# SBUF pools laid out anew: TensorE's operands at multiples of 1024 bytes, the small tables in a pool of their own

## The chip, the core and the metric

The kernel runs on one core of a Trainium2 chip. The metric is device time in microseconds (us), the median over several runs. One further run was taken with the hardware profiler on; its trace is what is read below. In that trace PE is TensorE (PEld its weight loads), DVE is VectorE, ACT is ScalarE, POOL is GpSimd, SP is SyncE. `L185` is line 185 of the kernel. A matmul's *stationary* operand is the one that is loaded as weights, its *moving* operand the one that is streamed through.

## What is computed

One decoder layer, batch 1, 512 tokens, width 1024, float32. Two token mixers work side by side, dilated attention and a state-space model (SSM); their outputs are gated and projected, and a SwiGLU feed-forward network with 2816 hidden channels follows.

```
p = x @ w_in                    # q, k, v (3 groups x 8 heads x 64) | ssm input | gate logits
attn = merge of 3 dilated sliding-window attentions
y_s  = glu(gelu(s5_ssm(u)));    y_attn = attn @ w_attn_br;   y_ssm = y_s @ w_ssm_br
mixed = sigmoid(g0) * y_attn + sigmoid(g1) * y_ssm
h = layer_norm(alpha * x + mixed @ w_out)
x = layer_norm(alpha * h + (silu(h @ w_ff_gate) * (h @ w_ff_up)) @ w_ff_down)
```

## The kernel before

Every large product is made of three float32r matmuls (`mm3`, L184 to L187): each float32 operand is split into a high and a low part (ACT rounds the high part, L178, DVE takes the rest, L179), and hi x hi, hi x lo, lo x hi are accumulated in one PSUM bank. Nearly all of these matmuls have 128 stationary columns and 512 moving columns ("full width"); those of the v projection of two attention groups, of the first two feed-forward tiles and of the last down product have 256 ("half width"). By the program, 3,104 matmuls are full width. The order on every engine is written out by hand.

Weights stream from HBM in units of 128 x 2048 floats, each split into two pieces of 1024 columns. A piece sits in a slot, a pair of tiles `whi{n}`, `wlo{n}`. Slots 0, 1 and 2 belong to the pool `wp`. When the pool `pa` with the tiles of the mixers is closed (L1017), the pools `pb` and `bt` are opened in its place, and slots 3 and 4 are added from `pb` (L1022). From then on the slots are used in turn, 0, 1, 2, 3, 4. The stages that the prediction speaks of, in their order in time:

- **Branch products** (L990 to L1004): eight pieces of 24 matmuls; the first four have `gh`, `gl` as moving operand, the last four `ath` (twice in every three) and `atl`.
- **Output projection** (L1065 to L1117): `mix_hi`, `mix_lo` are stationary, the weights move; one of its eight pieces lies in slot 3.
- **Feed-forward, gate and up** (`fg`, L1125 to L1160): the weight pieces are stationary, the tokens `hh`, `hl` move. A piece makes one bank: 8 k-slices x 3 = 24 matmuls. The first four pieces are done in token halves (half width), the other 40 at full width: 960 matmuls.
- **Down product** (`dn`, L1172 to L1206): the hidden channels `ff` are stationary and the weight pieces move; 18 pieces of 4 token tiles x 2 column halves x 3 = 24 matmuls, then 72 more by token tile, 504 in all at full width; the last token tile is done at half width (`dq`).

A tile pool hands out addresses in the order in which its tiles are first asked for, and each pool begins where the one before it ends. Before, the pool `cp` holds only the identity matrix (512 bytes in a partition) behind a few constants, and `pa` mixes small tables (192, 64, 512, 640, ... bytes) with large tiles.

Of the kernel before, what the change touches and what calls it, by code (L numbers as in the profile page):

```python
# [10 lines left out]
F32 = mybir.dt.float32  # L11
# [5 lines left out]
P = 128  # L17
# [6 lines left out]
NH = 8  # L24
NPAIR = 4
NG = 32
NGP = 16
# [124 lines left out]
def emit(ctx, tc, i, out):  # L152
# [3 lines left out]
    cp = ctx.enter_context(tc.tile_pool(name="cp", bufs=1))  # L156
# [40 lines left out]
    pa_ctx = ExitStack()  # L197
    pa = pa_ctx.enter_context(tc.tile_pool(name="pa", bufs=1))
    at = pa_ctx.enter_context(tc.tile_pool(name="at", bufs=2))

    def big(n, name, dt=F32):
        return pa.tile([P, 2048], dt, tag=f"big{n}", name=name)

    def gat(n, name, dt=F32):
        return pa.tile([P, 2048], dt, tag=f"gat{n}", name=name)

    def home(n, name, dt=F32):
        return gat(n[1:], name, dt) if isinstance(n, str) else big(n, name, dt)
# [22 lines left out]
        w.add(i["w_dn"][f], 1)  # L231

    warm = at.tile([P, 512], F32, tag="tv", name="warm")
    wact = at.tile([P, 1], F32, tag="wact", name="wact", bufs=1)
    xr = [big(4 + j, f"x_raw{j}") for j in range(2)]
    xp = act_pair("x")
    wu = [big(j, f"wu_raw{j}").rearrange("p (k c) -> p k c", k=4) for j in range(2)]
    wup = [[home(j, f"wu{n}{j}", F32R).rearrange("p (k c) -> p k c", k=4) for j in js] for n, js in (("h", (3, 6)), ("l", (7, "g3")))]
    small = pa.tile([P, 3, NGP], F32, name="small")
    ident = cp.tile([P, P], F32, name="ident")  # L240

    act.dma_start(small, i["ssm_small"])
    dve.memset(warm, 0.0)
# [18 lines left out]

    rope = pa.tile([P, 2, 512], F32, name="rope")
    masks = pa.tile([P, 2, 256], F32, name="masks")
    bgate = pa.tile([P, 16], F32, name="bgate")
    prep = gat(0, "prep")
    sm = prep[:, 0:1024].rearrange("p (a r e) -> p a r e", a=2, r=2)
    zt = prep[:, 1024:2048]
    dmat = pa.tile([P, 8, 16], F32, name="dmat")
    sp.dma_start(sm, i["ssm_bc"])  # L270
    w.load()
    sp.dma_start(dmat, i["dmat"])
# [11 lines left out]
    def t16():  # L284
        return t16s[:, next(n16), :]
# [94 lines left out]
    def bc(a, n):  # L380
        return a.unsqueeze(2).broadcast_to([P, NGP, n])

    ptmp = pa.tile([P, 2, NGP, 4], F32, name="ptmp")

    def powers(t, eng):
        for n0 in (1, 2, 4):
# [6 lines left out]

    are, aim, ldt = (small[:, j, :] for j in range(3))
    dtt, er, cr, ci, den, w0, w1, w2, w3, w4 = (t16() for _ in range(10))
    pw = pa.tile([P, 2, NGP, 5], F32, name="pw")
    a4 = pa.tile([P, 2, NGP, 9], F32, name="a4")
    a32 = pa.tile([P, 2, NGP, 5], F32, name="a32")
    neg = pa.tile([P, 3, NGP], F32, name="neg")
    pwn = pa.tile([P, NGP, 4], F32, name="pwn")  # L400
    ar1, ai1 = pw[:, 0, :, 1], pw[:, 1, :, 1]
    la, lb = Later(dve), Later(dve)
    exp16(dtt, ldt, la)
# [90 lines left out]
            act.copy(pf[:, 512 * q : 512 * (q + 1)], b)  # L494

    kdr = dr.tile([NG, 16, 112], F32, name="kdr")
    zer = pa.tile([16, 1, 48], F32, name="zer")
    pool.memset(zer, 0.0)
    act.dma_start(kdr.rearrange("g h e -> h g e")[:, :, 0:48], zer.broadcast_to([16, NG, 48]))

# [73 lines left out]
            act.copy(ssm["s", r][:, :, 8 * m + half : 8 * m + 8 : 2].rearrange("p s g b -> p g b s"),  # L574
                     b.rearrange("p (g b s) -> p g b s", g=4, b=16))

    f1 = pa.tile([P, 2, 4, NGP], F32, name="f1")
    e1 = pa.tile([P, 2, NGP], F32, name="e1")
    e2 = pa.tile([P, 2, NGP], F32, name="e2")

    def scan():

# [104 lines left out]
        sp.dma_start(ssm["ych"].rearrange("p (q t) -> p q t", q=4), ydr.rearrange("(q p) t -> p q t", p=P))  # L687


    st = [pa.tile([P, 2, 4, NH], F32, name=f"st{j}") for j in range(2)]  # L690
    oa = [None, None]

    def qk_tile(dv, ws, g, hp, name, mid):
# [326 lines left out]
    pb = ctx.enter_context(tc.tile_pool(name="pb", bufs=1))  # L1020
    bt = ctx.enter_context(tc.tile_pool(name="bt", bufs=2))
# [5 lines left out]
    xn = [ffslot(f"xn{j}").rearrange("p (t d) -> p t d", t=2) for j in range(2)]  # L1027
    lnb = ffslot("lnb").rearrange("p (e d) -> p e d", e=2)
    hn = pb.tile([P, NTT, D], F32, name="hn")
    epsb = pb.tile([P, 1], F32, name="epsb")  # L1030
    pool.memset(epsb, -0.5)

    def rstd(mv):
# [261 lines left out]
def build(inputs):  # L1295
    import concourse.bacc as bacc

    a = {k: np.asarray(v) for k, v in inputs.items()}
    arrays = {f"in_{k}": np.ascontiguousarray(v) for k, v in {**layout(a), **constants()}.items()}
    nc = bacc.Bacc("TRN2", target_bir_lowering=False, num_devices=1)  # L1300
    aps = {k[3:]: nc.dram_tensor(k, v.shape, mybir.dt.from_np(v.dtype), kind="ExternalInput").ap()
           for k, v in arrays.items()}
    out = nc.dram_tensor("out_dram", (S, D), F32, kind="ExternalOutput").ap()
    with tile.TileContext(nc) as tc:
        with ExitStack() as ctx:
            with tc.manual_schedule():
                emit(ctx, tc, aps, out)
    return nc, arrays
# [8 lines left out]
```

## Time and profile before

| | |
|---|---|
| median of 3 runs | 880.92 us (880.84 to 882.03) |
| profiled execution, its own time | 883.05 us |
| its span, first to last instruction | 881.3 us |
| PE busy | 865.2 us, 98% of the span, 4814 matmuls |
| DVE, ACT, POOL busy | 496.4, 294.3, 26.0 us |
| mean granted TensorE clock | 0.994 |

Matmuls overlap: a row's duration is longer than the distance to the next one's start. What a matmul costs in a row of many is the distance from start to start, here called its pitch.

### The profile page before, as it was taken

What the parts mean: (1) busy time and instruction counts of PE and PEld (TensorE: products, weight loads), DVE (VectorE), ACT (ScalarE), POOL (GpSimd) and SP (SyncE); (2) the same over time, 40 slices, a digit from 0 to 9 for tenths busy, and PEclk for the clock granted to TensorE, in tenths of its full rate; (3) what the DMA queues carried; (4) which work ended last, traced back from release to release, by engine and by line L of the source; (5) the groups of instructions that cost most, each with busy time, mean ns of one, the idle gap of its engine ahead of it and who ended that gap; (6) DMA issues with size and microseconds to landing.
All of it is one profiled execution on the core that took longest, in us unless ns stands there. A gap on an engine that the chain in (4) does not pass through costs nothing.

```text
span 881.3 us, 11787 instructions
## 1 busy us (share of the span) xinstructions
PE 865.2 (98%) x4814; PEld 715.7 (81%) x4814; DVE 496.4 (56%) x950; ACT 294.3 (33%) x479; POOL 26.0 (3%) x27
## 2 busy tenths in 40 slices
PE   9999999999999999998999999999999999999995
PEld 6878888888778897876788898888888888888885
DVE  7966899874664635366766864444444444222236
ACT  5363222254443343553233232222222222211110
POOL 0000000000000000000000410000000000000004
PEclk9999999999999999998999999999999999999999
DMA  9823421324221212112216222222222222322204
GB/s 330 188 80 103 119 96 63 129 64 134 93 96 49 96 48 100 55 43 95 96 49 267 115 95 102 95 97 97 96 94 96 98 96 95 142 95 97 92 1 96
DMA packets 23864, 90.11 MB, mean 102 GB/s; under 512 B 5722, under 2 KB 10330, under 8 KB 14722
## 3 DMA queue, kind: packets, MB, share of 16 engines
q1 hardware_dynamic: 22226, 86.87, 29.1%
q10 hardware_dynamic: 1584, 2.48, 0.8%
q8 instruction: 38, 0.62, 0.3%
q14 instruction: 16, 0.13, 0.0%
HBM read 84.92 MB, written 4.42 MB: 101 GB/s over the span
## 4 chain that ended last, share of the span: by engine, by line
PE 45%; issue 41%; DVE 8%; ACT 3%; POOL 2%; DMA 1%; SPq 0%; DVEq 0%; POOLq 0%; ACTq 0%
PE pg L185 3%; PE pg L186 3%; PE pg L187 3%; PE pv L185 3%; PE pu L548 3%; PE pv L187 3%; PE pv L186 3%; PE pk L185 3%; PE pq L185 3%; PE pq L187 2%; PE pk L187 2%; PE pq L186 2%; PE pk L186 2%; PE s L747 2%; DVE wlo L179 2%
## 5 line engine op out<-in xcount | busy, mean ns | idle before, releaser
L179 DVE TENSOR_TENSOR wlo<-raw,whi 128x1024 fp32r<-128x1024 f32 x134 | 164.1, 1228 | 203.4 <-ACT whi L178 203.2
L178 ACT CAST whi<-raw 128x1024 fp32r<-128x1024 f32 x134 | 139.6, 1046 | 217.5 <-PE dn L187 74.8
L185 PE MATMUL fg<-hh,whi 128*128 128x512 f32 (+1 forms) x384 | 143.5, 374 | 0.0
L187 PE MATMUL fg<-hh,wlo 128*128 128x512 f32 (+1 forms) x384 | 143.4, 373 | 0.0
L186 PE MATMUL fg<-hl,whi 128*128 128x512 f32 (+1 forms) x384 | 143.4, 373 | 0.0
L186 PEld LDWEIGHTS fg<-hl,whi 128*128 128x128 f32 x384 | 72.3, 188 | 13.3
L187 PEld LDWEIGHTS fg<-hh,wlo 128*128 128x128 f32 x384 | 72.3, 188 | 13.3
L185 PEld LDWEIGHTS fg<-hh,whi 128*128 128x128 f32 x384 | 72.3, 188 | 13.3
L185 PE MATMUL dn<-whi,ff 128*128 128x512 f32 x168 | 66.0, 393 | 0.0
L187 PE MATMUL dn<-whi,ff 128*128 128x512 f32 x168 | 65.9, 392 | 0.0
L186 PE MATMUL dn<-wlo,ff 128*128 128x512 f32 x168 | 65.8, 392 | 0.0
L185 PE MATMUL pg<-x_hi,whi 128*128 128x512 f32 x128 | 50.8, 397 | 0.0
L187 PE MATMUL pg<-x_hi,wlo 128*128 128x512 f32 x128 | 49.9, 390 | 0.0
L186 PE MATMUL pg<-x_lo,whi 128*128 128x512 f32 x128 | 49.9, 389 | 0.0
L181 ACT ACTIVATE ff<-fth 128x512 fp32r<-128x512 f32 x22 | 14.0, 635 | 101.6 <-DVE fth L297 101.6
L759 ACT ACTIVATE pt<-pt,st 128x256 f32<-128x256 f32 (+1 forms) x64 | 31.0, 485 | 47.1 <-DVE st L757 47.1
L297 DVE TENSOR_TENSOR fth<-fth,fg 128x512 f32<-128x512 f32 x22 | 15.1, 688 | 55.8 <-PE fg L187 55.6
L185 PE MATMUL pq<-x_hi,whi 128*128 128x512 f32 x96 | 37.9, 395 | 0.0
L185 PE MATMUL pk<-x_hi,whi 128*128 128x512 f32 x96 | 37.8, 394 | 0.0
L187 PEld LDWEIGHTS dn<-whi,ff 128*128 128x128 f32 x168 | 31.5, 188 | 7.3
L187 PE MATMUL pk<-x_hi,wlo 128*128 128x512 f32 x96 | 37.4, 390 | 0.0
L186 PE MATMUL pk<-x_lo,whi 128*128 128x512 f32 x96 | 37.4, 390 | 0.0
(254 smaller groups left out, 1564.7 us busy)
## 6 DMA issues: line engine op xcount, KB each, us to landing
raw<-in_w_in SPq DMA_DIRECT2D x26, 1024.0 KB, 4.8
raw<-in_w_gu SPq DMA_DIRECT2D x22, 1024.0 KB, 4.7
raw<-in_w_dn SPq DMA_DIRECT2D x11, 1024.0 KB, 4.8
raw<-in_w_br SPq DMA_DIRECT2D x4, 1024.0 KB, 4.7
raw<-in_w_out SPq DMA_DIRECT2D x4, 1024.0 KB, 4.7
raw<-in_w_glu SPq DMA_DIRECT2D x2, 1024.0 KB, 4.8
xn<-in_x SPq DMA_DIRECT2D x2, 1024.0 KB, 8.3
out_dram<-hn SPq DMA_DIRECT2D x13, 128.0 KB, 2.4
```

Of the source, the lines that this page charges most:

```text
L178: act.copy(hi, src)
L179: dve.tensor_tensor(lo, src, hi.bitcast(F32), op=ALU.subtract)
L181: act.mul(hi, src, scale)
L185: pe.matmul(dst, a[0], b[0], start=first, stop=False)
L186: pe.matmul(dst, a[0], b[1], start=False, stop=False)
L187: pe.matmul(dst, a[1], b[0], start=False, stop=last)
L297: eng.tensor_tensor(o, a, b, op=op)
L548: pe.matmul(bs[e], wk[a], xk[b], start=(k + a + b == 0), stop=(k == KT - 1 and a == 1))
L747: pe.matmul(banks[hh][:, 256 * j + 128 * c : 256 * j + 128 * (c + nk)], z[0][rows, hp, qs], z[1][rows, hp, 128 * k0 : 128 * (k0 + nk)], st ...
L759: act.activation(pt[:, :n], pt[:, :n], AF.Exp, bias=mneg, scale=-1.0, accum_out=zsum)
```

## The change

The instructions of PE, DVE, ACT and SP stay the same, in the same order and with the same waits; where tiles lie in SBUF changes. Three small tables (`pw`, `a32`, `e1`) move into `cp` ahead of the identity, so that `cp` ends at a round address and all pools after it begin there. All other small tables move from `pa` into a new pool `sa` behind `pa` and `at`. The one-column tile `epsb` moves from `pb` to `bt`, so that `pb`'s slots 3 and 4 follow at round addresses.

```diff
     at = pa_ctx.enter_context(tc.tile_pool(name="at", bufs=2))
+    sa = pa_ctx.enter_context(tc.tile_pool(name="sa", bufs=1))
+    pw = cp.tile([P, 2, NGP, 5], F32, name="pw")
+    a32 = cp.tile([P, 2, NGP, 5], F32, name="a32")
+    e1 = cp.tile([P, 2, NGP], F32, name="e1")
+    ident = cp.tile([P, P], F32, name="ident")
...
-    wact = at.tile([P, 1], F32, tag="wact", name="wact", bufs=1)
+    wact = sa.tile([P, 1], F32, name="wact")
...
-    small = pa.tile([P, 3, NGP], F32, name="small")
-    ident = cp.tile([P, P], F32, name="ident")
+    small = sa.tile([P, 3, NGP], F32, name="small")
...
-    bgate = pa.tile([P, 16], F32, name="bgate")
+    bgate = sa.tile([P, 16], F32, name="bgate")
...
-    dmat = pa.tile([P, 8, 16], F32, name="dmat")
+    dmat = sa.tile([P, 8, 16], F32, name="dmat")
...
-    epsb = pb.tile([P, 1], F32, name="epsb")
+    epsb = bt.tile([P, 1], F32, name="epsb", bufs=1)
```

`ptmp`, `a4`, `neg`, `pwn`, `zer`, `f1`, `e2` and `st` go from `pa` to `sa` in the same way.

Where the built programs place the tiles that TensorE reads (byte within a partition, and what is left over 128 and over 1024):

```
tile                            before   mod 128  mod 1024     after   mod 1024
ident                            16512         0       128     17920        512
whi0, wlo0 ... wlo2 (wp)         33408 ...     0       640     34816 ...      0
x, mix, ff7 to ff10 (ap_)        57984 ...     0       640     59392 ...      0
hh, hl, ff0 to ff6               90752 ...     0       640     92160 ...      0
gh                              162688         0       896    163840          0
ath (also zs, hst1, v1)         185024        64       704    182272          0
gl (also ut, q1)                194688         0       128    190464          0
whi3, wlo3, whi4, wlo4 (pb)     197280 ...    32       672    198656 ...      0
vt (at)                         215200        32       160    210944          0
pt (at)                         223392 ...    32       160    219136 ...      0
```

Slices of these tiles that a full-width matmul reads begin at multiples of 512 bytes from the tile's start (stationary) or 2048 (moving). Of the 3,104 full-width matmuls before, 700 have one operand that begins off a multiple of 128 bytes. Of the tiles before, none begins at a multiple of 256 bytes.

On POOL the waits stand elsewhere, since `epsb` now lies over other tiles than before. Its instructions from the last one of the mixers to the first layer normalization, before (`whl` is a table of the attention merge, `mva` the statistics of a token tile, `hn` its rows, `lnb` the scale and shift):

```order
L838 MEMSET whl 40x1024 [waits DMAHW2_49,DMAHW3_49,DMAHW1_49,DMAHW4_49,DMAHW0_49,DMAHW5_49,DVE_49,DMAHW6_49,PE_49,Activation_49]
L1031 MEMSET epsb 128x1 [waits DMAHW3_49,DMAHW2_49,DMAHW4_49,DMAHW1_49,DMAHW5_49,DMAHW0_49,DMAHW6_49,DVE_49,DMAHW7_49,PE_49,Pool_49]
L1035 ISA
L1035 TENSOR_TENSOR mva_4299<-mva_4299,epsb 128x1 [waits DVE_49,Pool_49]
L1059 TENSOR_TENSOR hn<-hn,lnb 128x512 [waits DMAHW2_49,Activation_49]
L1060 TENSOR_TENSOR hn<-hn,lnb 128x512 [waits Pool_49]
```

The same six on POOL in the changed program:

```order
L842 MEMSET whl 40x1024 [waits DMAHW2_49,DMAHW3_49,DMAHW1_49,DMAHW4_49,DMAHW0_49,DMAHW5_49,DVE_49,DMAHW6_49,PE_49,Activation_49]
L1035 MEMSET epsb 128x1 [waits DVE_49,PE_49]
L1039 ISA
L1039 TENSOR_TENSOR mva_4303<-mva_4303,epsb 128x1 [waits DVE_49,Pool_49]
L1063 TENSOR_TENSOR hn<-hn,lnb 128x512 [waits DMAHW3_49,DMAHW4_49,DMAHW2_49,DMAHW5_49,DMAHW1_49,DMAHW6_49,DMAHW0_49,DMAHW7_49,PE_49,Activation_49]
L1064 TENSOR_TENSOR hn<-hn,lnb 128x512 [waits Pool_49]
```

The waits for DMA queues moved from the memset to the first multiplication by `lnb`; that multiplication now waits for eight queues and PE beside ACT, instead of for one queue and ACT.

## Rows read from the trace of the kernel before

**Rows 1.** The page: span, and the busy time of each engine.
```profile
span 881.3 us, 11787 instructions
PE 865.2 (98%) x4814; PEld 715.7 (81%) x4814; DVE 496.4 (56%) x950; ACT 294.3 (33%) x479; POOL 26.0 (3%) x27
```

**Rows 2.** Windows: length, busy time of PE, PEld, DVE, ACT, POOL, clock, DMA share, GB/s.
```profile
530.32:750.52 220.20, 220.20 (x962) 180.24 (x961) 88.75 (x101) 62.44 (x80) 0.00 (x0) 1.00 0.28 99
750.52:866.58 116.06, 116.06 (x506) 94.55 (x504) 35.24 (x42) 21.06 (x21) 5.88 (x5) 1.00 0.24 82
```

**Rows 3.** Timeline, PE: start and duration (us); first matmuls of down pieces, end.
```profile
750.52 0.40 PE L185 MATMUL dn<-whi,ff 128*128 128x512 f32 x1
...
756.13 0.39 PE L185 MATMUL dn<-whi,ff 128*128 128x512 f32 x1
...
761.73 0.40 PE L185 MATMUL dn<-whi,ff 128*128 128x512 f32 x1
...
767.20 0.39 PE L185 MATMUL dn<-whi,ff 128*128 128x512 f32 x1
...
772.64 0.39 PE L185 MATMUL dn<-whi,ff 128*128 128x512 f32 x1
...
778.08 0.40 PE L185 MATMUL dn<-whi,ff 128*128 128x512 f32 x1
...
783.69 0.39 PE L185 MATMUL dn<-whi,ff 128*128 128x512 f32 x1
...
866.58 0.28 PE L185 MATMUL dq<-whi,ff 128*128 128x256 f32 x1
```

**Rows 4.** Timeline, PE: first matmuls of feed-forward pieces, full width.
```profile
530.32 0.40 PE L185 MATMUL fg<-hh,whi 128*128 128x512 f32 x1
...
541.51 0.39 PE L185 MATMUL fg<-hh,whi 128*128 128x512 f32 x1
...
712.12 0.39 PE L185 MATMUL fg<-hh,whi 128*128 128x512 f32 x1
...
717.56 0.39 PE L185 MATMUL fg<-hh,whi 128*128 128x512 f32 x1
```

**Rows 5.** Timeline, PE: branch products, fourth piece, fifth piece, first after the eighth.
```profile
432.25 0.39 PE L185 MATMUL b<-gh,whi 128*128 128x512 f32 x1
...
437.69 0.40 PE L185 MATMUL b<-ath,whi 128*128 128x512 f32 x1
...
460.08 0.40 PE L185 MATMUL wo<-whi,mix_hi 128*128 128x512 f32 x1
```

**Rows 6.** Timeline, PE: output projection, the piece in slot 3, first after it.
```profile
476.44 0.40 PE L185 MATMUL wo<-whi,mix_hi 128*128 128x512 f32 x1
...
482.05 0.40 PE L185 MATMUL wo<-w,mix_hi 128*128 128x512 f32 x1
```

**Rows 7.** Timeline, PE: feed-forward at half width, a piece in slot 4, the end.
```profile
505.67 0.28 PE L185 MATMUL fg<-hh,whi 128*128 128x256 f32 x1
...
508.51 0.28 PE L185 MATMUL fg<-hh,whi 128*128 128x256 f32 x1
...
529.96 0.28 PE L185 MATMUL fg<-hh,whi 128*128 128x256 f32 x1
```

**Rows 8.** POOL's semaphore waits at L1031: duration ns min/median/max.
```profile
L1031 POOLq EVENT_SEMAPHORE  x5: 42/43/79316, 389.5 to 469.1; - x5
```

**Rows 9.** Timeline: the first multiplication by the scale, its rows' first transposes.
```profile
492.12 1.30 POOL L1059 TENSOR_TENSOR hn<-hn,lnb 128x512 f32<-128x512 f32 x1 [1.12 <-ACT hn L1058]
...
495.69 0.38 PE L1085 MATMUL hb<-ident,hn 128*128 128x128 f32 x2
```

**Rows 10.** Timeline, PE: the first matmul on loaded data.
```profile
5.68 0.79 PE L548 MATMUL pu<-x_hi,wuh 128*128 128x512 f32 x1 [0.35 <-ACT wuh L178]
```

More of the change, by code (lines that the diff above doesn't have):

```diff
@@ L381, in bc @@
         return a.unsqueeze(2).broadcast_to([P, NGP, n])
-    ptmp = pa.tile([P, 2, NGP, 4], F32, name="ptmp")
+    ptmp = sa.tile([P, 2, NGP, 4], F32, name="ptmp")
     def powers(t, eng):
@@ L395, in emit @@
     dtt, er, cr, ci, den, w0, w1, w2, w3, w4 = (t16() for _ in range(10))
[L396 to L400, printed above, removed]
+    a4 = sa.tile([P, 2, NGP, 9], F32, name="a4")
+    neg = sa.tile([P, 3, NGP], F32, name="neg")
+    pwn = sa.tile([P, NGP, 4], F32, name="pwn")
     ar1, ai1 = pw[:, 0, :, 1], pw[:, 1, :, 1]
@@ L496, in emit @@
     kdr = dr.tile([NG, 16, 112], F32, name="kdr")
-    zer = pa.tile([16, 1, 48], F32, name="zer")
+    zer = sa.tile([16, 1, 48], F32, name="zer")
     pool.memset(zer, 0.0)
@@ L575, in state_inputs @@
                      b.rearrange("p (g b s) -> p g b s", g=4, b=16))
-    f1 = pa.tile([P, 2, 4, NGP], F32, name="f1")
-    e1 = pa.tile([P, 2, NGP], F32, name="e1")
-    e2 = pa.tile([P, 2, NGP], F32, name="e2")
+    f1 = sa.tile([P, 2, 4, NGP], F32, name="f1")
+    e2 = sa.tile([P, 2, NGP], F32, name="e2")
     def scan():
@@ L687, in turn_y @@
         sp.dma_start(ssm["ych"].rearrange("p (q t) -> p q t", q=4), ydr.rearrange("(q p) t -> p q t", p=P))
-    st = [pa.tile([P, 2, 4, NH], F32, name=f"st{j}") for j in range(2)]
+    st = [sa.tile([P, 2, 4, NH], F32, name=f"st{j}") for j in range(2)]
     oa = [None, None]
```

## The prediction

> **What bounds the kernel now.** I read the page's busy times first: PE is busy for 865.2 of 881.3 us [rows 1], so nothing but TensorE's own pace can give more than the 16 us in which it waits. [...]
>
> In the down product a piece is 24 full-width matmuls. The distances between the first matmuls of seven pieces in a row are 5.61, 5.60, 5.47, 5.44, 5.44, 5.61 us [rows 3]: two long pieces, three short ones, and long again. The period is five, as many as there are weight slots. The long ones are the pieces in slots 3 and 4, whose tiles begin 32 bytes past a multiple of 128, the short ones those in slots 0 to 2, which begin at a multiple of 128. In the down product the slot is the moving operand. In the feed-forward stage it is the stationary one, and the same is seen: the first two full-width pieces (slots 3 and 4) take 11.19 us, 233.1 ns a matmul, a piece in slot 2 takes 5.44 us, 226.7 ns [rows 4]. In the branch products the pieces with `gh` and `gl` (left over 128: 0) run at 5.44 us, those with `ath` (left over: 64) at (460.08 - 437.69) / 4 = 5.60 us [rows 5]. So before the change a full-width matmul has a clean pitch of 5.44 / 24 = 226.7 ns, and one of some 233.4 ns where either operand begins off a multiple of 128 bytes. I call these clean and ragged.
>
> **The change part by part.** After it no operand that a full-width matmul reads is ragged. I take the clean pitch for all of them, since it is what the same instructions show with the same neighbours a few us away. Each term is the measured length of a stretch less its count times 226.67 ns; this takes in the few matmuls after a ragged piece that are late too (the 5.47 us above).
>
> - Feed-forward at full width: 750.52 - 530.32 = 220.20 us [rows 3, 4] for 960 matmuls; clean 217.60. Gain 2.60.
> - Down product: 866.58 - 750.52 = 116.06 us [rows 3] for 504; clean 114.24. Gain 1.82.
> - Branch products with `ath`: 22.39 us [rows 5] for 96; clean 21.76. Gain 0.63.
> - Output projection, the piece in slot 3: 482.05 - 476.44 = 5.61 us [rows 6] for 24; clean 5.44. Gain 0.17.
> - Half width: the piece in slot 4 takes 508.51 - 505.67 = 2.84 us for 24, 118.3 ns each, while three clean ones take 530.32 - 529.96 = 0.36 us, 120 ns each [rows 4, 7]. Here ragged is no slower, and a hair quicker. Two such pieces lose 0.04 us each if they go to 120 ns: loss 0.08.
>
> The sum is 2.60 + 1.82 + 0.63 + 0.17 - 0.08 = 5.14 us. It is counted on PE, and PE waits for nothing in these stretches, so it comes off the end in full; the work that feeds them has room, since the short pieces show the feeding keep up at 5.44 us. All else on PE (projections, attention, SSM) runs with operands whose remainder over 128 is 0 already, or with transposes of 128 columns; I cost it at nothing.
>
> The waits that moved on POOL: `epsb` waits for less, the first multiplication by `lnb` for eight DMA queues and PE. The tiles behind those waits were given up before 469 us, where before the memset had passed the same waits; so all that is added is the passing of some four waits, 43 ns each by the median [rows 8], 0.2 us. They pass while POOL is idle anyway, 1.12 us until ACT is done [rows 9]. Queued behind the multiplication is the one that adds the shift, and the transposes of these rows wait for that, 3.6 us later [rows 9]. Without the cover the price would be 0.2 us. Cost: nothing.
>
> DMA: every large tile's destination moves. PE depends on transfers alone only before 5.68 us, when its first matmul on data starts [rows 10]. The trace has no transfer of the same kind to another remainder, so I bound this by a tenth of those 5.68 us either way, 0.6 us, and take zero; later transfers are not on PE's path.
>
> The bound that matters is that of the clean pitch itself. Before, no tile begins at a multiple of 256 bytes, so the trace cannot show whether 226.7 ns still holds a price for the left-over 128. [...] From above I know a ragged matmul, 6.7 ns more. I take no change, because clean pieces with remainders 128, 640 and 896 over 1024 (`gl`, the weights, `gh`) all show the same 5.44 us [rows 4, 5].
>
> [...]
>
> **The rivals.** [...]
>
> *It doesn't do what it says.* The extra 6.7 ns belongs to where the slots lie (the top of the partition, from 185,024 up) and not to the remainder. Slots 3 and 4 stay at the top after the change, so nothing is gained: 880.9 us. [...] For it: the ragged tiles all lie high. Against it: `gl` lies at 194,688, above `ath`, and is read by 8 of the 24 matmuls of the piece that takes 5.44 us [rows 5].
>
> *Slower: the two reads meet.* After the change stationary and moving operand both begin at the same place within 1024 bytes. If weight load and streaming then get into each other's way at the ragged price, the 2,404 full-width matmuls that are clean now pay 6.7 ns, 16.1 us: 897.0 us. It decides as soon as it costs more than 5.14 us / 3,104 = 1.7 ns a matmul. For it: both operands' placement moves a pitch, so the reads seem coupled. Against it: before, weights and tokens begin at 640 over 1024 alike, and that is the clean case [rows 4].
>
> **How the numbers follow.** The profiled execution took 883.05 us, its span of 881.3 and 1.75 around it; the forecast for it is 877.9 us. The median of the runs shown is 880.92, 2.13 lower; I take the 5.14 us off that: 875.8 us. Chances: forecast 0.78, second step 0.12, no change 0.06, slower 0.04. A difference of 0.2% (1.8 us) is about what a measurement of this kernel can tell from none; so faster 0.90, same 0.06, slower 0.04. The forecast's own range is 874.2 to 877.4, from the 0.6 us of the first transfers and 1 us for how the matmuls settle after each break. The 8-in-10 range reaches up to the no-change case, 881.2, and down to 871.0, which is a second step of 1.6 ns a matmul; it leaves out most of that rival and the slower one.
>
> **What the profile of the changed kernel would show.** Right: down pieces all 5.44 us apart with no period of five; full-width feed-forward 217.6 us long; the branch products with `ath` 21.8 us; matmuls of these groups at 0.39 us, none at 0.40; half-width pieces near 2.88 us; POOL's first multiplication by `lnb` still at ACT's heels. [...] Wrong on placement: slots 3 and 4 still at 5.6 us. Wrong on the other side: projection pieces over 5.5 us, where they are clean now.

## The result, and the profile after

The changed kernel takes 877.07 us in the median (875.81 to 877.77, 6 runs); the kernel before, run beside it, 881.83 us (880.84 to 883.02, 6 runs). The ratio is 0.9945, with a 95% interval of 0.9932 to 0.9958: faster by about half a per cent. The forecast, 875.8 against 880.92 us, was a ratio of 0.9942. The 877.07 us are 1.3 above the forecast; the kernel before was 0.9 us slower in this set of runs than in the one that the forecast started from.

The page of the profiled execution, whose own time was 876.89 us, answers to [rows 1]:

```profile
span 875.1 us, 11787 instructions
PE 859.7 (98%) x4814; PEld 715.8 (82%) x4814; DVE 496.0 (57%) x950; ACT 294.3 (34%) x479; POOL 26.0 (3%) x27
```

PE is busy for 5.5 us less with the same 4,814 matmuls; the others do the same work in nearly the same time. The windows of the two stages of [rows 2] (length, busy time of PE, PEld, DVE, ACT, POOL, clock, DMA share, GB/s):

```profile
528.89:746.52 217.63, 217.63 (x963) 180.25 (x961) 88.71 (x101) 62.49 (x80) 0.00 (x0) 1.00 0.29 100
746.52:860.76 114.24, 114.24 (x506) 94.62 (x504) 35.21 (x42) 21.12 (x21) 5.76 (x5) 1.00 0.24 83
```

The clock is 1.00 as before, PE is again busy without a break (217.63 of 217.63 us, 114.24 of 114.24), and the stages are 2.57 and 1.82 us shorter: 217.63 us is 960 matmuls of 226.7 ns, 114.24 is 504 of them. The timeline of PE (start and duration): the first matmuls on data [rows 10] and of the v projection; the pieces of the branch products and the output projection [rows 5, 6]; half and full width of the feed-forward stage [rows 4, 7]; the down pieces [rows 3]:

```profile
4.97 1.88 PE L553 MATMUL pu<-x_hi,wuh 128*128 128x512 f32 x4
...
27.55 0.39 PE L185 MATMUL pv<-x_hi,whi 128*128 128x512 f32 x1
...
431.48 0.39 PE L185 MATMUL b<-gh,whi 128*128 128x512 f32 x1
436.92 0.39 PE L185 MATMUL b<-ath,whi 128*128 128x512 f32 x1
458.68 0.39 PE L185 MATMUL wo<-whi,mix_hi 128*128 128x512 f32 x1
...
475.02 0.39 PE L185 MATMUL wo<-whi,mix_hi 128*128 128x512 f32 x1
480.46 0.39 PE L185 MATMUL wo<-w,mix_hi 128*128 128x512 f32 x1
504.14 0.28 PE L185 MATMUL fg<-hh,whi 128*128 128x256 f32 x1
507.01 0.28 PE L185 MATMUL fg<-hh,whi 128*128 128x256 f32 x1
528.89 0.40 PE L185 MATMUL fg<-hh,whi 128*128 128x512 f32 x1
...
746.52 0.39 PE L185 MATMUL dn<-whi,ff 128*128 128x512 f32 x1
751.96 0.39 PE L185 MATMUL dn<-whi,ff 128*128 128x512 f32 x1
757.40 0.39 PE L185 MATMUL dn<-whi,ff 128*128 128x512 f32 x1
762.84 0.39 PE L185 MATMUL dn<-whi,ff 128*128 128x512 f32 x1
768.28 0.39 PE L185 MATMUL dn<-whi,ff 128*128 128x512 f32 x1
773.72 0.39 PE L185 MATMUL dn<-whi,ff 128*128 128x512 f32 x1
...
860.76 0.28 PE L185 MATMUL dq<-whi,ff 128*128 128x256 f32 x1
```

The period of five is gone: every down piece takes 5.44 us. The four branch pieces with `ath` take 21.76 us, the output piece in slot 3 5.44 us. The half-width piece of slot 4 went from 2.84 to 2.87 us, a little slower, as forecast.

Because the order of the work is the same, starts of the same matmul in the two traces can be subtracted, and the whole difference can be put in its places. The start of the v projection before, for the first row:

```profile
28.30 0.39 PE L185 MATMUL pv<-x_hi,whi 128*128 128x512 f32 x1
```

| first matmul of | before | after | gained so far | gained since the row above | forecast |
|---|---|---|---|---|---|
| v projection | 28.30 | 27.55 | 0.75 | 0.75 | 0 |
| branch products with `ath` | 437.69 | 436.92 | 0.77 | 0.02 | 0 |
| output projection | 460.08 | 458.68 | 1.40 | 0.63 | 0.63 |
| its piece in slot 3 | 476.44 | 475.02 | 1.42 | 0.02 | 0 |
| the piece after it | 482.05 | 480.46 | 1.59 | 0.17 | 0.17 |
| feed-forward, half width | 505.67 | 504.14 | 1.53 | -0.06 | 0 |
| feed-forward, full width | 530.32 | 528.89 | 1.43 | -0.10 | -0.08 |
| down product | 750.52 | 746.52 | 4.00 | 2.57 | 2.60 |
| its half-width part | 866.58 | 860.76 | 5.82 | 1.82 | 1.82 |
| end of the span | 881.3 | 875.1 | 6.2 | 0.4 | 0 |

The five terms came to 5.09 us, forecast 5.14. The other 1.1 us of the two profiled executions lies mostly ahead of 28 us (0.71 of it before the first matmul on data) and in the last 15 us, where nothing was forecast; experiment 1 shows whether the layout did it.

On POOL, the rows that answer to [rows 9]:

```profile
488.92 0.93 POOL L1039 TENSOR_TENSOR mva<-mva,epsb 128x1 f32<-128x1 f32 x1 [58.79 <-DVE mva L296]
490.96 1.30 POOL L1063 TENSOR_TENSOR hn<-hn,lnb 128x512 f32<-128x512 f32 x1 [1.12 <-ACT hn L1062]
```

The multiplication by `lnb`, which now has the eight queues and PE to wait for beside ACT, still starts 1.12 us after the work before it, when ACT is done: moving the waits cost nothing.

### The profile page after: what moved, and what is told of

Its sections match the earlier page's. It is cut to its first block, busy times and chain, and to the rows that moved or that the text cites. A ratio compares the mean times of both kernels' runs of the same rounds, so it can differ in the third digit from the quotient of the medians.

```text
span 875.1 us, 11787 instructions
## 1 busy us (share of the span) xinstructions
PE 859.7 (98%) x4814; PEld 715.8 (82%) x4814; DVE 496.0 (57%) x950; ACT 294.3 (34%) x479; POOL 26.0 (3%) x27
## 4 chain that ended last, share of the span: by engine, by line
PE 46%; issue 40%; DVE 8%; ACT 3%; POOL 2%; DMA 1%; DVEq 0%; SPq 0%; POOLq 0%; ACTq 0%
PE pg L185 3%; PE pg L186 3%; PE pg L187 3%; PE pv L185 3%; PE pv L187 3%; PE pv L186 3%; PE pu L553 3%; PE pk L185 3%; PE pq L185 3%; PE pq L186 2%; PE pq L187 2%; PE pk L187 2%; PE pk L186 2%; PE s L751 2%; DVE wlo L179 2%
## 5 line engine op out<-in xcount | busy, mean ns | idle before, releaser
L186 PE MATMUL pq<-x_lo,whi 128*128 128x512 f32 x96 | 37.4, 390 | 0.0
L187 PE MATMUL pq<-x_hi,wlo 128*128 128x512 f32 x96 | 37.4, 390 | 0.0
```

Of the source, the lines that this page charges most:

```text
L186: pe.matmul(dst, a[0], b[1], start=False, stop=False)
L187: pe.matmul(dst, a[1], b[0], start=False, stop=last)
```

## The experiments

In all of them every engine has the instructions and the waits of the changed kernel, but for POOL's waits in experiment 2, which stand as before, and one wait on ACT in experiment 5. Experiments 1, 2 and 6 have a median of several runs, all others a single run. The time of the changed kernel to compare with is 877.07 us.

**1. The one-line part alone.** The kernel before, with only `epsb` moved. Slots 3 and 4 then begin at 640 over 1024, as the other large tiles do; `ath` stays 64 bytes off.

```diff
-    epsb = pb.tile([P, 1], F32, name="epsb")
+    epsb = bt.tile([P, 1], F32, name="epsb", bufs=1)
```

> The kernel before with one line of the change: the one-column table epsb goes from pool pb to bt, so that slots 3 and 4 begin at 640 over 1024 (0 over 128); all else stays, the branch operand ath still at 64 over 128. If the remainder over 128 sets the pitch (theory A): full-width feed-forward 217.6 us, down product to dq 114.3 us, the piece of the output projection in slot 3 5.44 us, the four branch pieces with ath still 22.4 us; together 2.60 + 1.82 + 0.17 - 0.08 = 4.5 us less than before, ratio 0.995. If the pitch needs multiples of 256 or more (B): nothing, ratio 1.000. If it is the place high in the partition (C): nothing, ratio 1.000.

Measured: 876.85 us, ratio 0.9944 (0.9927 to 0.9960). The windows of the two stages, and PE's timeline:

```profile
529.41:747.04 217.63, 217.63 (x962) 180.25 (x961) 88.72 (x101) 62.44 (x80) 0.00 (x0) 1.00 0.29 100
747.04:861.28 114.24, 114.24 (x505) 94.62 (x504) 35.22 (x42) 21.13 (x21) 5.76 (x5) 1.00 0.24 83
```

```profile
27.60 0.39 PE L185 MATMUL pv<-x_hi,whi 128*128 128x512 f32 x1
...
436.89 0.40 PE L185 MATMUL b<-ath,whi 128*128 128x512 f32 x1
...
459.28 0.40 PE L185 MATMUL wo<-whi,mix_hi 128*128 128x512 f32 x1
```

Both stages have the length that they have after the whole change, to 0.01 us, and the branch products with `ath` keep their 22.39 us. So one line carries nearly all of the gain. The first row settles where the 0.75 us came from: until the mixers are closed, this kernel's layout is that of the kernel before, and its v projection starts at 27.60 us too. That start varies from run to run (27.12 to 28.17 us in the nine other runs below, with no order by layout).

**2. The rest without that line.** The changed kernel with `epsb` back in `pb`: `ath` clean, slots 3 and 4 at 32 over 1024.

> The changed kernel without that line: epsb back in pb, so that slots 3 and 4 begin 32 past a multiple of 1024; everything else at multiples of 512 or more. Theory A: the branch pieces with ath 21.76 us, down pieces again 5.44 and 5.61 us with a period of five; 0.63 us less than before, ratio 0.9993, not to be told from 1. If the rest of the change gives the 1 us by which the profiled run fell more than forecast (6.2 against 5.1), ratio 0.998.

Measured: 881.69 us, ratio 0.9996 (0.9987 to 1.0006). The same windows:

```profile
530.09:750.29 220.20, 220.20 (x962) 180.33 (x961) 88.74 (x101) 62.41 (x80) 0.00 (x0) 1.00 0.28 99
750.29:866.35 116.06, 116.06 (x506) 94.60 (x505) 35.22 (x42) 21.06 (x21) 5.88 (x5) 1.00 0.24 82
```

220.20 and 116.06 us are exactly those of [rows 2], though the other tiles that these two stages read have all been moved to multiples of 1024 bytes. The four branch pieces with `ath` take 459.53 - 437.77 = 21.76 us, as after the whole change:

```profile
437.77 0.39 PE L185 MATMUL b<-ath,whi 128*128 128x512 f32 x1
...
459.53 0.39 PE L185 MATMUL wo<-whi,mix_hi 128*128 128x512 f32 x1
```

The 0.6 us that `ath` gives shows in its stage; a whole run can't tell it.

**3. Which remainder counts: every operand moved together.** An unused tile at the end of `cp` with 16 columns moves all operands of the full-width matmuls by 64 bytes; with 8 columns, by 32. (The identity matrix, which only transposes read, stays.)

```diff
+    pad = cp.tile([P, 16], F32, name="pad")
```

> The changed kernel with an unused tile of 64 bytes at the end of cp, so that every operand of TensorE begins 64 past a multiple of 512 or more; no instruction and no wait differs. Theory A1, each operand's own remainder over 128 counts: all 3,104 full-width matmuls at some 232 to 233 ns, 17 to 21 us more than the changed kernel, some 896 us. Theory A2, only the difference of the two operands' remainders counts (how the weight load and the streaming meet): 226.7 ns everywhere, 877 us.

> The changed kernel with 32 unused bytes at the end of cp: every operand of TensorE begins 32 past a multiple of 512 or more, so that the difference of any two operands' remainders over 128 stays 0. If the difference alone counts (A2): 226.7 ns at full width everywhere, 120 at half width, 877 to 879 us as with 64 bytes. If 32, which is off a multiple of 64 too, is worse than 64 for an operand by itself (A1): some 233 ns, 895 us.

Measured: 878.64 and 877.24 us, one run each. The windows, for 64 and for 32 bytes:

```profile
530.35:747.98 217.63, 217.63 (x963) 180.25 (x961) 88.73 (x101) 62.45 (x80) 0.00 (x0) 1.00 0.28 100
```

```profile
528.86:746.49 217.63, 217.63 (x963) 180.19 (x961) 88.75 (x101) 62.38 (x80) 0.00 (x0) 1.00 0.29 100
```

No operand of a full-width matmul begins at a multiple of 128 bytes now, and the stage is as clean as before. An operand's own remainder does not count, at 32 and 64 bytes (217.63 us with 0, 32 and 64 alike); how the operands stand to each other does, as experiment 4 shows.

**4. Which difference counts: the low slots alone moved.** Slots 0 to 2 are moved by 32, 64, 128 or 256 bytes; a gap behind them makes 1024 bytes of the two together, so that all else keeps its remainders over 1024. (The raw weights, which TensorE does not read, move with the slots.) The diff for 32 bytes; the others have 16 and 240, 32 and 224, 64 and 192 columns:

```diff
+    pad = cp.tile([P, 8], F32, name="pad")
...
+    pad_w = wp.tile([P, 248], F32, tag="pad_w", name="pad_w")
```

> The changed kernel with 32 unused bytes ahead of pool wp and 992 behind its tiles: slots 0, 1 and 2 (and the raw weights) begin 32 past a multiple of 1024, slots 3 and 4 and all other operands stay at multiples of 512 or more. Theories A1 and A2: the 2,268 full-width matmuls that read these slots at 233.4 ns, in projections, branches, feed-forward and down alike; down pieces now 3 long and 2 short; 15 us more than the changed kernel, 892 us. Theory C (place): low slots do not pay, 877 us.

> As the run with slots 0 to 2 at 32, but at 64 past a multiple of 1024 (960 bytes behind them). The difference is 64 for the same 2,268 full-width matmuls. If any difference that is no multiple of 128 pays alike: 233 ns, 888 us. If what counts repeats every 64 bytes: 226.7 ns, 877 us. Half width (the v projection of two groups, 384 matmuls): 118.5 ns as at 32, or 120 to 121.

> The same with 128 (896 bytes behind): the difference is 128 over 256, which neither kernel has anywhere. If what counts repeats every 128 bytes: 226.7 ns everywhere, 877 us. If every 256: some 2,268 matmuls off their pitch, slower by 11 us as at 32, or quicker, since a difference of 0 need not be the best one.

> The changed kernel with slots 0 to 2 moved by 256 bytes, all else in place: the distances of 32, 64 and 128 bytes cost some 11 us. Theory: the pitch is clean when the two offsets differ by a multiple of 256. Then all pieces stay at 5.44 us and the time at 877.1 us. Rival: the period is 512 or more; then the pieces in slots 0 to 2 take 5.6 us in every stage and the time is about 888 us.

Measured, one run each: 888.35, 887.47, 888.22 and 876.57 us. The windows of both stages for 32, 64, 128 and 256 bytes:

```profile
534.28:755.78 221.50, 221.50 (x962) 180.28 (x961) 88.78 (x101) 62.44 (x80) 0.00 (x0) 1.00 0.28 99
755.78:872.14 116.36, 116.36 (x505) 94.55 (x504) 35.22 (x42) 21.04 (x21) 5.87 (x5) 1.00 0.24 81
```

```profile
534.21:755.86 221.65, 221.65 (x963) 180.37 (x961) 88.81 (x101) 62.44 (x80) 0.00 (x0) 1.00 0.28 99
755.86:871.18 115.32, 115.32 (x505) 94.62 (x504) 35.24 (x42) 21.05 (x21) 5.86 (x5) 1.00 0.24 82
```

```profile
534.40:755.81 221.41, 221.41 (x963) 180.63 (x961) 88.79 (x101) 62.39 (x80) 0.00 (x0) 1.00 0.28 99
755.81:872.00 116.19, 116.19 (x506) 94.59 (x505) 35.24 (x42) 21.04 (x21) 5.85 (x5) 1.00 0.24 81
```

```profile
528.54:746.17 217.63, 217.63 (x962) 180.19 (x961) 88.71 (x101) 62.47 (x80) 0.00 (x0) 1.00 0.29 100
746.17:860.41 114.24, 114.24 (x505) 94.59 (x504) 35.22 (x42) 21.13 (x21) 5.76 (x5) 1.00 0.24 83
```

Differences of 32, 64 and 128 bytes all cost (11.28, 10.40 and 11.15 us in the whole time), one of 256 costs nothing (876.57 against 877.07 us). At 32 bytes 11.3 us came where 15 were expected. The half-width matmuls of v gave 1.1 us back (see experiment 6), and the gate projections went from 227.6 ns a matmul in the mean to 233.3, 5.7 more and not 6.7; the rest stays open. That refutes place as the cause, since the slots low in the partition are now the ragged ones, and it shows in stages where pieces were always clean: with the slots 32 bytes off, the pieces of the gate projections (`pg`) are 5.60 us apart on PE's timeline,

```profile
89.20 0.40 PE L185 MATMUL pg<-x_hi,whi 128*128 128x512 f32 x1
...
94.80 0.40 PE L185 MATMUL pg<-x_hi,whi 128*128 128x512 f32 x1
```

where the changed kernel has them 5.44 us apart:

```profile
87.87 0.39 PE L185 MATMUL pg<-x_hi,whi 128*128 128x512 f32 x1
...
93.31 0.39 PE L185 MATMUL pg<-x_hi,whi 128*128 128x512 f32 x1
```

The price is not the same everywhere: with the slots 64 bytes off, the down pieces from them take 5.49 to 5.51 us and not 5.60. PE's timeline of that run, the first two pieces from slots 3 and 4, the next three from slots 0 to 2:

```profile
755.86 0.39 PE L185 MATMUL dn<-whi,ff 128*128 128x512 f32 x1
...
761.33 0.39 PE L185 MATMUL dn<-whi,ff 128*128 128x512 f32 x1
...
766.77 0.40 PE L185 MATMUL dn<-whi,ff 128*128 128x512 f32 x1
...
772.28 0.39 PE L185 MATMUL dn<-whi,ff 128*128 128x512 f32 x1
...
777.77 0.39 PE L185 MATMUL dn<-whi,ff 128*128 128x512 f32 x1
...
783.26 0.40 PE L185 MATMUL dn<-whi,ff 128*128 128x512 f32 x1
```

**5. Whose difference: low parts alone moved.** `wlo` of all slots and `hl` are moved by 32 bytes, `whi` and `hh` stay at multiples of 256. The order of the three matmuls makes two theories part in the feed-forward stage. (Gaps behind the low parts, not shown in the diff, bring the next tile to a multiple of 256 again. `ff` has nine buffers in place of eleven, since `hl` has tiles of its own; one transfer that ACT issues waits for one matmul more than before.)

```diff
+            self.views["pad", j] = pool.tile([P, 8], F32, tag=f"pad{j}", name=f"pad{j}", bufs=1)
...
-        return pb.tile([P, 2048], dt, tag="ff", name=name, bufs=11)
+        return pb.tile([P, 2048], dt, tag="ff", name=name, bufs=9)
...
+    pad_h = pb.tile([P, 8], F32, name="pad_h")
+    hls = [pb.tile([P, 2048], F32R, name=f"hl{j}") for j in range(2)]
```

> The changed kernel with 32 bytes ahead of the low parts only: `wlo` of all five slots and `hl` begin 32 bytes past a multiple of 256, `whi`, `hh` and all else at a multiple of 256. A feed-forward product is three matmuls, (stationary, moving) = (whi, hh), (whi, hl), (wlo, hh). Theory `own pair`: a full-width matmul pays 6.7 ns when its own two operands differ by other than a multiple of 256 bytes. Then the second and third of every three pay: feed-forward at full width 960 x (226.7 + 6.7 x 2/3) = 221.9 us. Theory `next load`: it pays when its moving operand differs so from the stationary operand of the matmul behind it, which is loaded while it streams. The pairs are then (hh, whi), (hl, wlo), (hh, whi), all of difference 0: 217.6 us, nothing paid. In the other full-width stages with slots (some 2,050 matmuls) both theories have one in three pay, about 4.6 us; in the projections, where the weights are stationary, `own pair` has the third of every three long and `next load` the second. The whole time from the 877.1 us of the changed kernel: own pair 886, next load 881.7.

Measured: 890.26 us, above both expectations. The window of feed-forward at full width:

```profile
534.37:757.31 222.94, 222.94 (x962) 180.27 (x961) 88.82 (x101) 62.33 (x80) 0.00 (x0) 1.00 0.28 98
```

222.94 us for 960 is 232.2 ns a matmul: neither 217.6 nor 221.9 us. Worked out from the starts of all of them, (whi, hh) has a mean pitch of 233.3 ns, the longest of the three (the others have 231.5 and 231.9), although both its operands begin at a multiple of 256. In the gate projections, where one matmul in three has a ragged operand, the three pitches are 232.6, 238.1 and 228.7 ns by their place in the order, 233.1 in the mean, where experiment 4 has 233.3 with all three off: one odd read in three costs about as much as three. The longest is the second, as `next load` has it, but the other two aren't clean. So both theories fall as they stand. What a matmul pays is decided neither by its own pair alone nor by its moving operand and the next load alone; in these runs a row of matmuls is clean only while all its reads begin at one remainder over 256.

**6. The other way round, for half width.** At half width the ragged pitch is the quicker one (118.5 against 121.4 ns for v, with the slots 32 bytes off in experiment 4). The slot tiles get 64 more columns, and the weight pieces of half-width products begin 8 or 16 columns in.

```diff
-        hi = pool.tile([P, 1024], F32R, tag=f"whi{j}", name=f"whi{j}_{n}", bufs=1)
+        hi = pool.tile([P, 1088], F32R, tag=f"whi{j}", name=f"whi{j}_{n}", bufs=1)
...
+        o = 0
+        if n < len(STEPS) and STEPS[n][0] == "v" and STEPS[n][1]:
+            o = 8
+        elif N_FF <= n < N_FF + 4:
+            o = 16
+        return hi[:, o : o + 1024], lo[:, o : o + 1024]
```

> The changed kernel with the slot tiles 256 bytes longer, so that the weight pieces of half-width products can begin further in: 32 bytes for the v projection of groups 1 and 2, 64 bytes for the first four feed-forward pieces; all full-width pieces stay at a multiple of 256. Theory: a half-width matmul is quicker when its two operands' offsets differ by no multiple of 256 bytes (118.5 against 121.4 ns for v with a difference of 32, 119.0 against 120.7 ns for feed-forward with 64). Then 375 x 2.9 + 140 x 1.7 ns = 1.3 us come off: 875.8 us where the changed kernel took 877.1, ratio to the kernel before 0.993. Rival: those pitches came with something else of the shifted layouts, and the time stays at 877.1, ratio 0.9945.

Measured: 875.21 us (874.61 to 875.69, 6 runs), ratio to the kernel before 0.9922 (0.9909 to 0.9935). It is the lowest time of all the kernels here. Windows over the first v piece of group 1 (with the short matmuls behind it), busy time of PE and PEld with v alone; the changed kernel:

```profile
169.47:175.22 5.75, 3.04 (x25) 2.83 (x24) 0.00 (x0) 1.00 0.51 182
```

and this one:

```profile
169.10:174.78 5.68, 2.96 (x25) 2.76 (x24) 0.00 (x0) 1.00 0.53 185
```

0.07 us less in each of 16 such pieces is 1.1 us; feed-forward at half width went from 24.75 us (504.14 to 528.89) to 24.37 (502.59 to 526.96). Together that is 1.5 us where 1.3 were expected; the spans differ by 1.9, and 0.4 of that is there at the start of the v projection already (27.12 against 27.55 us). The two ratios' intervals overlap a little, so that this version beats the changed kernel is shown by its stages rather than by the whole time.

## Why the prediction was right, step by step

**What bounds the kernel** held: PE's busy time fell by 5.5 us and the span by 6.2; no other engine took over as the bound. That PE waits for nothing in the two long stages shows in their windows, before [rows 2] and after: it is busy for the whole of each, at clock 1.00.

**The terms** held to 0.03 us each: 2.57 for 2.60, 1.82, 0.63, 0.17, and -0.10 for -0.08. The 0.03 missing in the feed-forward stage is the setting-in after half width: 217.63 us where 960 times 226.67 ns are 217.60, and the first piece takes 5.47 us. Of the signs that the prediction named, one holds but for a few: 957 of the 960 feed-forward matmuls and all 504 of the down product have 0.39 us, three have 0.40.

**The clean pitch itself** held. It is 226.7 ns with all operands at 0, 32, 64 or (before) 128 over 256 alike, and in no run are the full-width windows of the two stages shorter than at that pitch (217.62 and 114.24 us at the least). The second step that the prediction gives a chance of 0.12, a clean pitch that falls further after the change, did not come: the short down pieces take 5.44 us before, and all take 5.44 us after. Nor does any run show the 1.6 ns of it that set the lower end of the 8-in-10 range.

**The reason given for ragged was wrong**, though it gave the right set of matmuls: "where either operand begins off a multiple of 128 bytes". That it gave the right set, and with it the right sum, was luck of this layout. A multiple of 128 neither is needed (experiment 3) nor does it suffice (128 bytes in experiment 4). Before, everything clean lay at 128 over 256 (640, 896 and 128 over 1024), slots 3 and 4 at 160 and `ath` at 192: the two rules could not be told apart in that trace. After the change all operands lie at 0 over 256, where both rules give the clean pitch. For the same reason the three remainders that were called on for an unchanged clean pitch, 128, 640 and 896, were one and the same place over 256, and bore less than they seemed to; and that no tile lay at a multiple of 256 did not matter (5.44 us a piece either way).

**It doesn't do what it says** fell: slots 3 and 4 still lie at the top and run at 5.44 us, and in experiment 4 the slots at the bottom run at 5.60.

**Slower: the two reads meet** fell as to sign and was right in what spoke for it: the pitch depends on how the two operands lie to each other, but lying alike is the cheap case (226.7 ns, against 233.3 in experiment 4). All at one remainder over 1024 is as clean as before (5.44 us a piece).

**Moved waits and transfers** cost nothing, as costed. The 1.1 us outside the terms is no effect of the change as far as the runs show: 0.7 of it comes in experiment 1 with the old layout at that time, and the tail from the half-width down product to the end of the span is 14.7 us before, 14.4 after, and again 14.6 in the kernel with all operands 64 bytes on. What varies there stays open.

## What to carry to other kernels

Where PE is busy without a break, read the distance between the starts of equal matmuls, piece by piece: here its period of five, as many as the slots that are used in turn, pointed at where the slots lie. For rows of 512-column float32r matmuls, each with its own weight load, place all operands of a row at the same remainder over 256 bytes: here that gave 226.7 ns a matmul, and in the mean of a row up to 233.3 without it. The remainders 0, 32, 64 and 128, alike for all, were equally good (226.7 ns); differences of 32, 64 and 128 cost (10.4 to 11.3 us in the whole time), others below 256 were not tried alone. One small tile ahead of a large one in the same pool is enough to lose it: here 4 bytes of `epsb`. Before moving everything, look for the one tile that breaks the pattern: here a single line gave a ratio of 0.9944 and the whole change 0.9945.

## What the runs showed of the hardware

In these runs a price of up to some 6.6 ns in the mean, 3% of a full-width matmul, is paid in rows of matmuls whose operands' start addresses differ modulo 256 bytes (233.3 against 226.7 ns). Moving the weights in slots 0 to 2 alone by 32 bytes lengthens the feed-forward stage from 217.63 to 221.50 us, and moving the tokens with them by as much leaves it at 217.63. Why the place of the one operand matters to the other, no run shows.

The size of the price differs from case to case here. With the slots 64 bytes off as the stationary operand, the feed-forward stage pays 4.02 us; as the moving one, the down product pays 1.08 us, where 32 and 128 bytes cost 2.12 and 1.95. It is not the operand alone, though: before the change `ath` was a moving operand 64 bytes off too, beside `atl`, which was in place, and its pieces paid in full (5.60 us). What sets the size stays open.

At half width the sign turns in these runs: with the slots off by 32, 64 and 128 bytes (experiment 4), the half-width matmuls of v are 118.5, 119.0 and 120.6 ns apart in the mean, in place 121.4 ns (from the starts in the four traces). The clean pitch there, some 120 ns, is more than half of 226.7 ns.
